# One fewer block-product pair in the first half-FFN, modulation weights loaded once for two conditions, and HGRN's states placed later, in a two-layer backbone on one core

## The chip, the cores and the metric

The kernel runs on one core of one Trainium2 chip, as one program. The metric is device time in microseconds, from the start of the program to its end, all loads from HBM and the stores of the result included. Times are medians of several runs.

## The reference, cut to what matters

Two layers work on a latent stream of 512 tokens and a context stream of 256 tokens, 1024 features each. A layer is a half-step FFN, a token mixer (HGRN2 in layer 0, a gated chunk MLP in layer 1) and a second half-step FFN. Each sub-layer's input is modulated, and its output is normalised, by rows of a modulation matrix product: nine chunks of 1024 values a layer, for the condition `c` of the latents (called "x" in the kernel) and, where context is needed, for `c_ctx` of the context (called "c").

```python
def modulation(cond, w_mod, b_mod):
    m = jax.nn.silu(cond) @ w_mod + b_mod          # w_mod: 1024 x 9*1024
    return m.reshape(m.shape[:-1] + (N_MOD, D_MODEL))
def modulate(x, m, k):
    return x * (1 + m[..., 3 * k + 1, :]) + m[..., 3 * k, :]
def post_norm_update(x, y, m, k, g, b):
    return layer_norm(DN_ALPHA * x + m[..., 3 * k + 2, :] * y, g, b)
def swiglu(h, w_in, w_out):                        # w_in: 1024 x 5632, w_out: 2816 x 1024
    gate, up = jnp.split(h @ w_in, 2, axis=-1)
    return (jax.nn.silu(gate) * up) @ w_out
...
        x = macaron_half_ffn(x, mx, 0, ...)        # chunks 0, 1, 2 for the latents
        ctx = macaron_half_ffn(ctx, mc, 0, ...)    # chunks 0, 1, 2 for the context
        hx = modulate(x, mx, 1)                    # chunks 3, 4
        yx, yc = hgrn2_mixer(hx, modulate(ctx, mc, 1), ...)
        x = post_norm_update(x, yx, mx, 1, ...)    # chunk 5
        x = macaron_half_ffn(x, mx, 2, ...)        # chunks 6, 7, 8
```

The mixer's scan has eight heads, two directions and 64-token chunks; each direction starts on the latents from the state that the context left.

## The kernel before

All products are float32, made from split operands: a value is a high part and a rest. `split` (L134 to L136) makes the high part on ACT (L135) and the rest on DVE (L136). `unit` (L139) loads one weight unit of 128x1024, 512 KB, into one of three `raw` buffers (L141) and splits it into one of six `w` buffers; the raw buffer is free when DVE's subtraction has read it. `mm3` (L146) issues three matmuls for each product of split operands (L148, L149, L150).

**The first half-FFN's input side** has 22 pairs of output blocks of 128 (gate and up). Three pairs run while the modulated input `xm` is still being made: the loop over the eight feature blocks k loads the modulation chunks 1 and 0 (`mw`, L1008) and one block of x (`xt`, three buffers, L1011), makes the dot products on DVE (L170), modulates on ACT (L1026), splits, copies the modulated block into spare `h` buffers for later use (L1039, two ACT copies of 128x256) and issues the matmuls. The other 19 pairs are made in `FeedSums.rest` (L766): first `plain` pairs, 48 matmuls of 512 columns each (`plain_pair`), then pairs by block products (`seven`, L673): seven products of 256 columns in place of eight, 84 matmuls of 256 columns, with four sums of weight halves on DVE and combinations of the results on DVE and ACT. During the plain pairs DVE and ACT also make the summed input blocks `f` that the block products need (`sum_steps`). Before, 9 pairs are plain and 10 are by blocks.

**The modulation rows** that are needed later are computed in the background. `mod_task` (L175) is a generator: each of its eight steps loads 512 KB of modulation weights (`mraw`, two buffers, L179) and makes a dot product on DVE for each condition it was given (L170, tile `junk`); after the last it finishes the chunk. Chunks 2, 5, 8 are gates: they go over a PE transpose (`pg`) and a store to HBM. `mod_step(n)` (L242) gives the queue of tasks n steps of credit, and is called after each pair or weight unit; `made(key)` (L255) runs as many steps as are missing. The loads go on SP's queue, which issues in order, as all loads and stores here do: a load that waits for its buffer holds all that is behind it.

**The stages, in order of time**: the start (`psf` matmuls while `xm` is made), the plain pairs, the block pairs, the output side of the first half-FFN for the latents (`OutPhase`, called x-out below), the input and output side of the same FFN for the context (ctx-in: 22 pairs of 48 matmuls of 256 columns; ctx-out: 22 units of 12 matmuls of 512 columns), HGRN's values, HGRN's heads, and what follows. The out phase of layer 0's second half-FFN (called (0,2) out phase below) calls `scraps` (L225) to queue modulation chunks (1,1) and (1,0) on other buffers (`rawu`).

**HGRN** runs eight heads in a loop (L1336 and on) that works on the projections of head h and on the scan of head h-1. `latent_states` (L1281) makes the three state products `pkl` of a direction; they need `kT`, a copy on ACT (L1235) of transposes that PE made just before. `gated` (L1324) transposes the normalised output `on` of a head (`pto`), which DVE makes at L1321.

The order of each engine's instructions comes from a scheduler that goes by the program's text; `tc.issue_after(i)` keeps an instruction behind i in that order.

Of the kernel before, what the change touches and what calls it, by code (L numbers as in the profile page):

```python
# [18 lines left out]
P = 128  # L19
D = 1024  # L20
KD = D // P
# [49 lines left out]
def backbone_kernel(  # L71
# [153 lines left out]
    def scraps(sp, l, chs, small=None):  # L225

        if small is None:
            s, small = (sp.tile([P, D], F32, tag="e", name="e", bufs=2) for _ in range(2))
        else:
            s, small = small[:, :D], small[:, D:]  # L230
        nc.sync.dma_start(s, cond[CI_OF["x"]].partition_broadcast(P))
        nc.scalar.activation(s, s, AF.Silu)
        small = Scraps(sp, small, "rawu")
        for ch in chs:
            queue_mod(small, {"x": s}, l, ch, ["x"])
# [751 lines left out]
    with sbuf(name="hp", bufs=1) as hp, sbuf(name="modp", bufs=1) as modp:  # L987
# [5 lines left out]
        with sbuf(name="first", bufs=1) as fp:  # L993
# [19 lines left out]

            staged, fed = 0, feed(0)
# [6 lines left out]
            for k in range(KD):  # L1021
# [15 lines left out]
                for p in range(2):  # L1037
                    b = f0.blocks[p, k // 2] if k % 2 else f0.block(p, k // 2)
                    nc.scalar.activation(b[:, k % 2, :], xf[:, p * 2 * P : (p + 1) * 2 * P], AF.Copy)  # L1039
# [4 lines left out]
                if k == 0:  # L1044
                    for _ in first:
                        pass
                elif k < 4:
                    f0.load((2, 2, 1)[k - 1])
            products(KD - 1, staged)
        nc.sync.dma_start(lnT, ln_T)  # L1050
        srow["c"] = silu_row(modp, "c")
        for ch, c in ((2, "x"), (1, "c"), (0, "c"), (4, "x"), (3, "x"), (2, "c"), (4, "c"), (3, "c")):
            queue_mod(modp, srow, 0, ch, [c])
        for l, ch in ((0, 5), (0, 7), (0, 6), (0, 8), (1, 2)):
            queue_mod(modp, srow, l, ch, ["x"])
        f0.enter()
        f0.sums()
        with sbuf(name="sp0", bufs=1) as sp:
            hget = f0.rest(hp, sp, 0.5, 9, 3.5)
        xcp = L0.enter_context(swap("xcp"))  # L1060
        xmc = new_xm(xcp, "xmc", TC)
        with bpools() as bp:
# [14 lines left out]
            ).run(bp, context_operand, 1.4)  # L1077
            hget = f1.rest(hp, 1.4)
# [8 lines left out]
            for l, ch in ((0, 8), (1, 2)):  # L1087
                made((l, ch, "x"))
# [3 lines left out]
    with sbuf(name="hgo", bufs=1) as hgo, ExitStack() as late:  # L1092
# [4 lines left out]
        with sbuf(name="hg", bufs=1) as hg:  # L1097
# [241 lines left out]
            for h in range(NH + 1):  # L1339
# [16 lines left out]
                if done:  # L1356
                    with tc.issue_after(last.ins):
                        gated(*done)
                if prev:
# [4 lines left out]
                    latent_states(h - 1, 1, r1, kT1)  # L1364
                if h < NH:
                    q, _ = proj_silu(h, 0, "q")
                    for r in (n0, n1):
                        queries(r, q)
                else:
                    op.lead(0, 2)  # L1370
                if prev:
# [22 lines left out]
    with sbuf(name="sp2", bufs=1) as sp, sbuf(name="hp2", bufs=1) as hp, bpools() as bp:  # L1394
# [11 lines left out]
        scraps(sp, 1, (1, 0))  # L1406
        op.run(bp, None, 1)
# [226 lines left out]
```

## Time and profile before

| | |
|---|---|
| median of 3 runs | 2460.67 us (2459.02 to 2461.65) |
| profiled execution | 2460.02 us, of which the trace's span is 2458.3 us |
| PE busy | 2413.8 us, 98% of the span |
| DVE, ACT busy | 2009.9 us (82%), 1190.7 us (48%) |
| DMA | 378.64 MB, mean 154 GB/s |
| start, plain pairs, block pairs | 54.2, 98.1, 102.2 us |
| x-out, ctx-in, ctx-out | 121.3, 141.7, 64.4 us |
| HGRN's heads 2 to 7 | 224.0 us |

Busy time of PE includes time in which matmuls overlap in the pipeline, so the share of 98% does not say that PE runs at its densest. The distance between the starts of two matmuls does: where nothing waits it is constant for a shape. A stage ends where the next one's first matmul starts.

### The profile page before, as it was taken

Reading aid. Unit: us, or ns where it says so; the run is one execution under the profiler, and the core shown is the slowest. Engines: PE = TensorE matmul, PEld = TensorE weight load, DVE = VectorE, ACT = ScalarE, POOL = GpSimd, SP = SyncE. Lnnn points to the kernel's source line nnn. Section 1 sums busy time; section 2 is a strip of 40 time slices with the busy share of each in tenths; the row PEclk is TensorE's granted clock in tenths of the full one; section 3 lists DMA queues with packets and bytes.
Section 4 is the critical chain, followed back from the end, with each engine's and each line's share of the span. In section 5 each row is a group of like instructions: output and inputs, shape, how many; then the busy total and the mean of one; then the engine's idle time right before and its main releaser. Section 6 shows DMA issues by size and latency. Waiting matters only on the chain.

```text
span 2458.3 us, 38793 instructions
## 1 busy us (share of the span) xinstructions
PE 2413.8 (98%) x15267; PEld 2198.5 (89%) x15267; DVE 2009.9 (82%) x3315; ACT 1190.7 (48%) x1878; POOL 35.0 (1%) x57
## 2 busy tenths in 40 slices
PE   7999999999999999999999999999999999999998
PEld 5889888988888888999988999988999988999987
DVE  7888889777388886988796988898899777998785
ACT  5335444444355542555643555534554443555641
POOL 0000000000000000000000000000000000000000
PEclk9999999999999999999999999999999999999999
DMA  8863866985211123433474333474422365333452
GB/s 316 276 206 120 284 213 219 314 301 178 86 61 61 47 66 116 138 119 106 130 239 139 112 114 108 147 253 139 133 89 87 114 222 173 135 121 104 138 160 80
DMA packets 110887, 378.64 MB, mean 154 GB/s; under 512 B 12856, under 2 KB 14192, under 8 KB 110704
## 3 DMA queue, kind: packets, MB, share of 16 engines
q1 hardware_dynamic: 110704, 376.17, 46.5%
q8 instruction: 119, 1.95, 0.3%
q14 instruction: 64, 0.52, 0.1%
HBM read 363.50 MB, written 12.61 MB: 153 GB/s over the span
## 4 chain that ended last, share of the span: by engine, by line
PE 72%; DVE 13%; DMA 7%; ACT 4%; issue 3%; POOL 1%; SPq 0%; DVEq 0%; POOLq 0%; ACTq 0%
PE y L150 7%; PE y L149 7%; PE y L148 7%; PE psc L148 6%; PE psc L150 6%; PE psc L149 6%; PE pse L150 3%; PE pse L148 3%; PE pse L149 3%; DVE w L136 3%; DMA mraw<-in_mod_w 3%; DMA raw<-in_ffn_w_out 2%; DVE junk L170 2%; ACT w L135 2%; DMA raw<-in_ffn_w_in 1%
## 5 line engine op out<-in xcount | busy, mean ns | idle before, releaser
L136 DVE TENSOR_TENSOR w<-raw,w 128x1024 fp32r<-128x1024 f32 (+3 forms) x447 | 495.2, 1113 | 142.8 <-ACT w L135 141.3
L135 ACT ACTIVATE w<-raw 128x1024 fp32r<-128x1024 f32 (+3 forms) x447 | 432.2, 970 | 370.5 <-DMA raw<-in_ffn_w_out 92.2
L150 PE MATMUL y<-w,hs 128*128 128x512 f32 x984 | 383.5, 390 | 2.4 <-DVE hs L136 2.3
L149 PE MATMUL y<-w,hs 128*128 128x512 f32 x984 | 382.9, 389 | 1.7 <-DVE w L136 1.7
L148 PE MATMUL y<-w,hs 128*128 128x512 f32 x984 | 383.7, 390 | 0.5 <-ACT w L135 0.5
L150 PEld LDWEIGHTS y<-w,hs 128*128 128x128 f32 x984 | 184.7, 188 | 44.1 <-DVE hs L136 5.6
L149 PEld LDWEIGHTS y<-w,hs 128*128 128x128 f32 x984 | 184.7, 188 | 40.4 <-DVE w L136 2.5
L148 PEld LDWEIGHTS y<-w,hs 128*128 128x128 f32 x984 | 184.8, 188 | 39.3 <-ACT w L135 0.7
L135 ACT ACTIVATE hs<-h 128x512 fp32r<-128x512 f32 (+1 forms) x220 | 123.8, 583 | 160.1 <-PE y L150 128.1
L148 PE MATMUL psc<-f,w 128*128 128x256 f32 x624 | 177.2, 284 | 1.6 <-ACT sc L734 1.5
L150 PE MATMUL pse<-f,w 128*128 128x256 f32 x624 | 176.9, 283 | 0.2 <-DVE w L136 0.2
L148 PE MATMUL pse<-f,w 128*128 128x256 f32 x624 | 176.7, 283 | 0.0
L150 PE MATMUL psc<-f,w 128*128 128x256 f32 x624 | 176.6, 283 | 0.0
L149 PE MATMUL pse<-f,w 128*128 128x256 f32 x624 | 176.6, 283 | 0.0
L149 PE MATMUL psc<-f,w 128*128 128x256 f32 x624 | 176.6, 283 | 0.0
L148 PE MATMUL psc<-xm,w 128*128 128x256 f32 x612 | 174.2, 285 | 0.9 <-ACT sc L734 0.9
L150 PE MATMUL psc<-xm,w 128*128 128x256 f32 x612 | 173.2, 283 | 0.0
L149 PE MATMUL psc<-xm,w 128*128 128x256 f32 x612 | 173.2, 283 | 0.0
L136 DVE TENSOR_TENSOR hs<-h,hs 128x512 fp32r<-128x512 f32 (+1 forms) x220 | 133.3, 632 | 42.3 <-ACT hs L135 41.9
L734 ACT ACTIVATE sc<-psc 128x256 f32<-128x256 f32 x218 | 83.5, 383 | 125.6 <-PE psc L150 119.6
L148 PE MATMUL psf<-xm,w 128*128 128x512 f32 (+1 forms) x384 | 127.4, 344 | 14.5 <-ACT xm L1032 11.1
L150 PE MATMUL psf<-xm,w 128*128 128x512 f32 (+1 forms) x384 | 130.4, 341 | 2.1 <-DVE w L136 2.1
(344 smaller groups left out, 6262.5 us busy)
## 6 DMA issues: line engine op xcount, KB each, us to landing
raw<-in_ffn_w_in SPq DMA_DIRECT2D x149, 512.0 KB, 4.7
raw<-in_ffn_w_out SPq DMA_DIRECT2D x110, 512.0 KB, 4.6
mraw<-in_mod_w SPq DMA_DIRECT2D x104, 512.0 KB, 5.0
rawu<-in_ffn_w_in SPq DMA_DIRECT2D x70, 512.0 KB, 3.7
rawu<-in_mod_w SPq DMA_DIRECT2D x64, 512.0 KB, 4.4
x<-x SPq DMA_DIRECT2D x36, 512.0 KB, 3.7
raw<-in_hg_wf SPq DMA_DIRECT2D x32, 512.0 KB, 3.6
raw<-in_cm_w_out SPq DMA_DIRECT2D x24, 512.0 KB, 4.5
```

Source lines behind the costliest of these rows:

```text
L135: latest_hi[0] = nc.scalar.activation(dst_hi, src, AF.Copy)
L136: latest[0] = nc.vector.tensor_tensor(dst_lo, src, dst_hi.bitcast(F32), ALU.subtract)
L148: nc.tensor.matmul(ps, ah, bh, start=start, stop=False, **kw)
L149: nc.tensor.matmul(ps, ah, bl, start=False, stop=False, **kw)
L150: return nc.tensor.matmul(ps, al, bh, start=False, stop=stop, **kw)
L170: nc.vector.scalar_tensor_tensor(junk, w[:, c], 1.0, s[:, c], ALU.mult, ALU.mult, dst[:, i : i + 1])
L734: nc.scalar.activation(sc[i], ps[:, :N2], AF.Copy, scale=scale)
```

## The change

- The first half-FFN takes 10 plain pairs and 9 by block products (before 9 and 10). The plain pairs give 2.7 steps of modulation each (before 3.5), the block pairs 0.4 (before 0.5).
- Chunks 2, 4 and 3 of layer 0 are queued once for both conditions ("xc"): one load of 512 KB serves two dot products. Before, each condition loaded them by itself. Chunk (0,8) is no longer in this queue; it is the first in the queue of the (0,2) out phase, whose rate goes from 1 to 1.25 steps a unit. The loads into `mraw` go from 104 to 72: 24 by sharing, 8 by the chunk that moves; those into `rawu` grow by these 8. The number of dot products is the same. The rates fall from 1.4 to 0.9 in x-out and from 1.4 to 0.5 in ctx-in; ctx-out keeps 0.5. At the end of ctx-in `made` runs the steps that chunks 5, 7 and 6 still lack. The loads of `mraw` that stand among ctx-out's weight loads go from 11 to 13, and nine of them stand among the first ten weight loads.
- At the start the copies into `h` (now `keep`) are made one k later, after the next block's high part.
- In HGRN, `latent_states` of the second direction is placed behind the first half of the next projection (`proj_silu`, tile `psq`); in the last turn of the loop, `gated` of head 6 is placed behind `op.lead(0, 2)`.

```diff
-    def scraps(sp, l, chs, small=None):
+    def scraps(sp, l, chs, small=None, first=None):
...
-        for ch in chs:
-            queue_mod(small, {"x": s}, l, ch, ["x"])
+        for key in ([first] if first else []) + [(l, ch) for ch in chs]:
+            queue_mod(small, {"x": s}, *key, ["x"])
...
+            def keep(k, x):
+                for p in range(2):
+                    b = f0.blocks[p, k // 2] if k % 2 else f0.block(p, k // 2)
+                    nc.scalar.activation(b[:, k % 2, :], x[:, p * 2 * P : (p + 1) * 2 * P], AF.Copy)
...
-                for p in range(2):
-                    b = f0.blocks[p, k // 2] if k % 2 else f0.block(p, k // 2)
-                    nc.scalar.activation(b[:, k % 2, :], xf[:, p * 2 * P : (p + 1) * 2 * P], AF.Copy)
+                if k:
+                    with tc.issue_after(latest_hi[0].ins):
+                        keep(k - 1, kept)
+                kept = xf
...
-        for ch, c in ((2, "x"), (1, "c"), (0, "c"), (4, "x"), (3, "x"), (2, "c"), (4, "c"), (3, "c")):
-            queue_mod(modp, srow, 0, ch, [c])
-        for l, ch in ((0, 5), (0, 7), (0, 6), (0, 8), (1, 2)):
+        for ch, conds in ((2, "xc"), (1, "c"), (0, "c"), (4, "xc"), (3, "xc")):
+            queue_mod(modp, srow, 0, ch, conds)
+        for l, ch in ((0, 5), (0, 7), (0, 6), (1, 2)):
             queue_mod(modp, srow, l, ch, ["x"])
...
-            hget = f0.rest(hp, sp, 0.5, 9, 3.5)
+            hget = f0.rest(hp, sp, 0.4, 10, 2.7)
...
-            ).run(bp, context_operand, 1.4)
-            hget = f1.rest(hp, 1.4)
+            ).run(bp, context_operand, 0.9)
+            hget = f1.rest(hp, 0.5)
...
-            for l, ch in ((0, 8), (1, 2)):
-                made((l, ch, "x"))
+            made((1, 2, "x"))
...
-                if done:
+                if done and h < NH:
                     with tc.issue_after(last.ins):
                         gated(*done)
...
-                    latent_states(h - 1, 1, r1, kT1)
                 if h < NH:
-                    q, _ = proj_silu(h, 0, "q")
+                    q, last = proj_silu(h, 0, "q")
+                    if prev:
+
+                        with tc.issue_after(last.ins):
+                            latent_states(h - 1, 1, r1, kT1)
                     for r in (n0, n1):
                         queries(r, q)
                 else:
+                    latent_states(h - 1, 1, r1, kT1)
                     op.lead(0, 2)
+                    gated(*done)
...
-        scraps(sp, 1, (1, 0))
-        op.run(bp, None, 1)
+        scraps(sp, 1, (1, 0), first=(0, 8))
+        op.run(bp, None, 1.25)
```

**On ACT, at the start**, from the first weight unit's first 128 columns on. Before:

```order
L135 ACTIVATE w<-raw 128x128
L1032 ACTIVATE xm<-xt,cols 128x512
L1039 ACTIVATE h<-xf 128x256 x2
L135 ACTIVATE w<-raw 128x896
L135 ACTIVATE w<-raw 128x1024
L1026 ACTIVATE xt<-xt,cols 128x512
```

Now:

```order
L135 ACTIVATE w<-raw 128x128
L1037 ACTIVATE xm<-xt,cols 128x512
L135 ACTIVATE w<-raw 128x896
L135 ACTIVATE w<-raw 128x1024
L1031 ACTIVATE xt<-xt,cols 128x512
L135 ACTIVATE w<-raw 128x1024
L135 ACTIVATE xm<-xt 128x512
L1017 ACTIVATE h<-xf 128x256 x2
```

The two copies into `h` of the first block moved from ahead of the first unit's other 896 columns to behind the second block's high part.

**On SP, in the middle of ctx-in**, among the weight loads of the context's input side. Before (buffer numbers are shown):

```order
L141 DMA raw_4389<-in_ffn_w_in 128x1024
L141 DMA raw_4419<-in_ffn_w_in 128x1024
L179 DMA mraw_4453<-in_mod_w 128x1024
L141 DMA raw_4457<-in_ffn_w_in 128x1024
L141 DMA raw_4487<-in_ffn_w_in 128x1024
L179 DMA mraw_4521<-in_mod_w 128x1024
L141 DMA raw_4525<-in_ffn_w_in 128x1024
L141 DMA raw_4555<-in_ffn_w_in 128x1024
L179 DMA mraw_4589<-in_mod_w 128x1024
L179 DMA mraw_4596<-in_mod_w 128x1024
```

Now:

```order
L141 DMA raw_4416<-in_ffn_w_in 128x1024
L179 DMA mraw_4544<-in_mod_w 128x1024
L141 DMA raw_4446<-in_ffn_w_in 128x1024
L141 DMA raw_4480<-in_ffn_w_in 128x1024
L179 DMA mraw_4676<-in_mod_w 128x1024
L141 DMA raw_4510<-in_ffn_w_in 128x1024
L141 DMA raw_4548<-in_ffn_w_in 128x1024
L141 DMA raw_4578<-in_ffn_w_in 128x1024
L416 DMA x_5046<-in_ctx_tok 128x1024
L141 DMA raw_4612<-in_ffn_w_in 128x1024
```

Four modulation loads to six weight loads became two to six, and the context's residual (`in_ctx_tok`) stands among them; before, both its loads stood at the end of the stage.

**On PE, in one HGRN head**, from the second direction's transposes (`ptk`) on; `pkl` are state products, `pssc` scores, `psq` the next head's projection. Before:

```order
L1233 MATMUL ptk<-ident,X 128x128 x3
L1287 MATMUL pkl<-v_5993,kT 128x128
L1287 MATMUL pkl<-v_5994,kT 128x128
L1287 MATMUL pkl<-v_5995,kT 128x128
L1256 MATMUL pssc<-B,X 128x128 x4
L1287 MATMUL pkl<-v_5996,kT 128x128
L1287 MATMUL pkl<-v_5995,kT 128x128
L1287 MATMUL pkl<-v_5994,kT 128x128
L148 MATMUL psq<-xm,w 128x512
```

Now (of the 24 matmuls of `psq` only the first and the last stand here):

```order
L1239 MATMUL ptk<-ident,X 128x128 x3
L1293 MATMUL pkl<-v_5847,kT 128x128
L1293 MATMUL pkl<-v_5848,kT 128x128
L1293 MATMUL pkl<-v_5849,kT 128x128
L1262 MATMUL pssc<-B,X 128x128 x4
L148 MATMUL psq<-xm,w 128x512
...
L150 MATMUL psq<-xm,w 128x512
L1293 MATMUL pkl<-v_5850,kT 128x128
L1293 MATMUL pkl<-v_5849,kT 128x128
L1293 MATMUL pkl<-v_5848,kT 128x128
```

The second group of `pkl` moved behind 24 matmuls of `psq`; the other 24 follow it.

## Rows read from the trace of the kernel before

**Rows 1.** The page: busy time of the engines as a share of the span, and the chain that ended last, by engine.

```profile
PE 2413.8 (98%) x15267; PEld 2198.5 (89%) x15267; DVE 2009.9 (82%) x3315; ACT 1190.7 (48%) x1878; POOL 35.0 (1%) x57
...
PE 72%; DVE 13%; DMA 7%; ACT 4%; issue 3%; POOL 1%; SPq 0%; DVEq 0%; POOLq 0%; ACTq 0%
```

**Rows 2.** Windows by stage: start and end in us, length, then busy us (and instructions) of PE, PEld, DVE, ACT and POOL, granted clock of PE, busy share of the DMA engines, GB/s. In order: plain pairs, block pairs, x-out, ctx-in, ctx-out, HGRN's heads 2 to 7.

```profile
54.20:152.30 98.10, 98.10 (x434) 81.04 (x434) 79.48 (x118) 30.57 (x39) 0.00 (x0) 1.00 0.79 259
152.30:254.50 102.20, 101.34 (x842) 100.91 (x841) 88.68 (x131) 59.65 (x103) 0.00 (x0) 1.00 0.44 144
254.50:375.80 121.30, 120.69 (x532) 98.85 (x531) 103.29 (x168) 50.64 (x73) 0.55 (x1) 1.00 0.76 253
375.80:517.50 141.70, 134.43 (x1090) 132.09 (x1088) 114.51 (x176) 58.15 (x82) 2.88 (x3) 0.99 0.81 275
517.50:581.90 64.40, 61.83 (x265) 49.05 (x266) 58.01 (x94) 38.20 (x65) 0.00 (x0) 1.00 0.86 289
...
722.70:946.70 224.00, 220.69 (x1359) 196.98 (x1358) 188.13 (x440) 110.99 (x173) 6.05 (x6) 1.00 0.19 57
```

**Rows 3.** Timeline of PE: start in us, us, engine, line, operation. Two starts of 512-column matmuls in the plain pairs, with four left out between them, and two of 256-column matmuls in the block pairs, with five left out.

```profile
99.97 0.39 PE L148 MATMUL psf<-xm,w 128*128 128x512 f32 x1
...
101.10 0.39 PE L150 MATMUL psf<-xm,w 128*128 128x512 f32 x1
...
199.76 0.28 PE L148 MATMUL psc<-f,w 128*128 128x256 f32 x1
...
200.48 0.28 PE L148 MATMUL psc<-f,w 128*128 128x256 f32 x1
```

**Rows 4.** PE's waits: what it waited for, us in total, times, longest. First ctx-in, then ctx-out.

```profile
PE psf L150 <- DVE w L136: 3.8, 6, 1.3
PE psf L148 <- ACT w L135: 2.8, 3, 1.6
...
PE y L150 <- DVE hs L136: 1.7, 3, 0.7
```

**Rows 5.** Windows, columns as in rows 2, of the change from x-out to ctx-in and of a stretch in ctx-out.

```profile
376.00:390.00 14.00, 14.00 (x122) 14.00 (x121) 13.28 (x26) 8.47 (x14) 2.88 (x3) 1.00 0.39 118
390.00:400.00 10.00, 9.52 (x81) 9.31 (x79) 9.92 (x19) 5.79 (x13) 0.00 (x0) 1.00 0.31 75
400.00:410.00 10.00, 7.89 (x53) 7.48 (x52) 9.52 (x14) 2.81 (x4) 0.00 (x0) 0.83 0.96 317
...
420.00:430.00 10.00, 8.53 (x69) 8.12 (x68) 9.43 (x16) 2.89 (x4) 0.00 (x0) 1.00 0.97 341
...
550.00:560.00 10.00, 8.88 (x38) 6.70 (x37) 10.00 (x19) 5.39 (x11) 0.00 (x0) 1.00 0.74 239
```

**Rows 6.** Waits of SP's queue in ctx-in: weight loads (L141) and modulation loads (L179), us in total, times, longest.

```profile
SPq L141 <- DVE w L136: 36.8, 21, 7.3
SPq L179 <- DVE junk L170: 27.7, 11, 7.4
```

**Rows 7.** DMA issues: count, KB each, median us from issue to landing. The first two in ctx-in, the third of the whole run (HGRN's weights, loaded where no modulation loads stand).

```profile
raw<-in_ffn_w_in SPq DMA_DIRECT2D x37, 512.0 KB, 5.5
mraw<-in_mod_w SPq DMA_DIRECT2D x27, 512.0 KB, 5.6
...
raw<-in_hg_wf SPq DMA_DIRECT2D x32, 512.0 KB, 3.6
```

**Rows 8.** DVE's instructions by line and form in ctx-in and ctx-out: count, busy us, mean ns, idle before.

```profile
L136 DVE TENSOR_TENSOR w<-raw,w 128x1024 fp32r<-128x1024 f32 x64 | 77.7, 1221 | 22.6 <-ACT w L135 22.0
L170 DVE SCALAR_TENSOR_TENSOR junk<-mraw,srow_x 128x1024 bf16<-128x1024 f32 x38 | 46.3, 1219 | 3.4 <-DMA mraw<-in_mod_w 3.1
L136 DVE TENSOR_TENSOR hs<-h,hs 128x256 fp32r<-128x256 f32 x44 | 17.2, 416 | 1.4 <-ACT hs L135 1.4
```

**Rows 9.** Timeline of PE in an HGRN head, and near the loop's end; in brackets the idle time before, and what ended it.

```profile
804.39 0.83 PE L1287 MATMUL pkl<-v,kT 128*128 128x128 f32 x6
805.06 1.06 PE L1256 MATMUL pssc<-B,X 128*128 128x128 f32 x8
806.49 0.94 PE L1287 MATMUL pkl<-v,kT 128*128 128x128 f32 x6 [0.38 <-ACT kT L1235]
...
942.05 0.63 PE L1327 MATMUL pto<-ident,on 128*128 128x128 f32 x4 [1.03 <-DVE on L1321]
```

**Rows 10.** PE's waits in HGRN's heads 2 to 7, columns as in rows 4.

```profile
PE pkl L1287 <- ACT kT L1235: 2.3, 6, 0.4
```

**Rows 11.** The start: timeline of ACT, DVE and SP, then PE's wait for the rest parts and SP's wait for an `xt` buffer.

```profile
10.91 0.71 ACT L1039 ACTIVATE h<-xf 128x256 f32<-128x256 f32 x2
12.49 1.09 DVE L136 TENSOR_TENSOR w<-raw,w 128x896 fp32r<-128x896 f32 x1 [0.76 <-ACT w L135]
...
41.17 0.63 ACT L135 ACTIVATE xm<-xt 128x512 fp32r<-128x512 f32 x1
44.89 0.63 ACT L135 ACTIVATE xm<-xt 128x512 fp32r<-128x512 f32 x1
46.23 1.06 ACT L161 ACTIVATE srow_c<-srow_c 128x1024 f32<-128x1024 f32 x1
...
SPq L1011 <- DVE xm L136: 12.1, 3, 4.4
```

**Rows 12.** Windows, columns as in rows 2, of a stretch in the (0,2) out phase.

```profile
1240.00:1280.00 40.00, 40.00 (x178) 33.14 (x177) 38.83 (x60) 16.58 (x23) 0.00 (x0) 1.00 0.83 270
```

More of the change, by code (lines that the diff above doesn't have):

```diff
@@ L1048, in backbone_kernel @@
                     f0.load((2, 2, 1)[k - 1])
+            keep(KD - 1, kept)
             products(KD - 1, staged)
```

## The prediction, made before the changed kernel was timed

> **What bounds the kernel now.** The page comes first: PE is busy for 98% of the span, and the chain that ended last is PE's for 72%, with 13% of DVE and 7% of DMA in it [rows 1]. So PE sets the time nearly everywhere. Next comes the pace of PE where nothing waits: five matmuls of 512 columns in 101.10 - 99.97 = 1.13 us, 0.226 us each, and six of 256 columns in 0.72 us, 0.120 us each [rows 3]. With these the windows by stage [rows 2] show where PE falls behind. The 432 matmuls of the plain pairs, 98.10/432 = 0.227 each, leave nothing to win. The block pairs need 840 x 0.120 = 100.8 of 102.20 us. Ctx-in needs 1090 x 0.120 = 130.8 of 141.70: 10.9 us are lost. Ctx-out needs 265 x 0.227 = 60.2 of 64.40: 4.2 are lost. These two are the worst stages that the change touches. HGRN's heads idle for 224.00 - 220.69 = 3.3 us. What ends PE's idle time in ctx-in is the weight split, on ACT and DVE [rows 4]; what stands behind that is a late load: the DMA engines are busy for 0.81 of the stage and 0.96 to 0.97 in parts of it [rows 2, 5], a weight load lands after 5.5 us where it took 3.6 without modulation loads around [rows 7], and SP holds weight loads for up to 7.3 us and modulation loads, with all that is behind them, for as long [rows 6].
>
> **The change part by part.** The sum is made against the profiled execution, 2460.02 us; the median of the three runs lies 0.65 above it, and that is added at the end.
>
> *One plain pair for a block pair.* PE gains 48 matmuls of 0.227 and loses 84 of 0.120: 10.9 - 10.1 = +0.8 us. By stages, 98.10/9 - 102.20/10 gives +0.7. DVE and ACT get lighter here, but PE does not wait for them in this stage, so that is worth nothing. I take +0.8. The Trainium skill ("TensorE: Matmul & The Clock Gate", section "Wait — 56ns, not 53.3ns?") gives 215.7 ns for a warm matmul of 512 columns, and by its formula one of 256 takes 109.2; an estimate from this page for the exchange is 10.35 - 9.17 = +1.2 us. The row's paces are both some 0.01 us longer than the page's, and the row decides.
>
> *Dots and loads around the plain and block pairs.* DVE is busy for 79.48 of 98.10 us with 3.5 dots a pair; by my count the 27 steps on 10 pairs now carry about 38 dots, 3.8 a pair. At 1.22 us a dot [rows 8] that is 0.4 us more in 10.9, from 0.81 to 0.84 busy. In the block pairs it goes from 0.5 dots to 0.8 a pair, from 0.87 to 0.90. PE's lead covers both: 0. If it does not, DVE's growth in the block pairs, 9 x 0.3 x 1.22 = 3.3 us, bounds the loss.
>
> *X-out.* In its first half a unit of 5.4 us now carries 1.8 dots (0.9 steps for two conditions) for 1.4: +0.49 us of DVE, which stands at 103.29 of 121.30, so 0.85 becomes 0.94 there. The nearest row of a DVE as full is ctx-out: 0.90 busy and 4.2 us lost, though part of that is the loads'. I take +0.5, from 0 to +3. The DMA share falls, from 0.76.
>
> *Ctx-in and ctx-out.* Ctx-in issues 27 modulation loads beside 37 weight loads [rows 7]; now some ten. A weight buffer goes round in landing + high part + rest, 5.5 + 1.0 + 1.2 = 7.7 us, three buffers give a unit every 2.6 us, and PE eats one in 24 x 0.120 = 2.88. That leaves 0.3 us a unit, which one hold of 7.3 us on SP uses up for 24 units. At the landing time of 3.6 a unit comes every 1.9 us, and PE can be led by all six `w` buffers. So I expect ctx-in's loss to go nearly whole. At its beginning, between 376 and 410, DVE is 95 to 99% busy and DMA at 0.31 to 0.39 up to 400: there it is DVE, with norms, operands and dots, that holds SP [rows 5]. By the order of SP's loads some seven modulation loads fewer stand around it now, 7 x 1.22 = 8.5 us of DVE; I leave 2 of the 10.9 us. In ctx-out the loads are not fewer (13 for 11), and nine fall on the first ten units, where DVE then needs 1.22 + 2 x 0.42 + 1.22 = 3.3 us for PE's 2.7. That deficit, 9 x 0.6 = 5 us, is met by the lead brought from ctx-in, up to five units or 13 us of PE. The loss at the start of the stage goes, that around the evacuation (DVE 10.00 of 10.00 at 550, rows 5) stays: 2.2 of the 4.2. Together -8.9 - 2.0 = -10.9 us. Bounds: -6 if the beginning's 4.3 us (2.6 idle and 1.7 of granted clock, 0.83 for ten us at 400) and all of ctx-out's stay; -14 if nearly nothing does.
>
> *HGRN.* The second `pkl` group follows 1.43 us after the start of eight matmuls (`pssc`) that at the pace of the group before (six in 0.67) take 0.89 [rows 9]: 0.54 lost, in six heads [rows 10], 3.2 us. Behind half of `psq`, 5.4 us later, `kT` has long been copied, and `pkl`'s results are needed only in the next head. The `pto` of the last turn waited 1.03 for `on` and now has `op.lead` ahead of it: 1.1. Together -4.3; bounds -5 and 0, see the rivals.
>
> *The start.* Taking the two copies out of ACT's way brings the first unit's rest part forward by up to 0.7 us: DVE waited 0.76 for it [rows 11]. Against that, an `xt` buffer now is read last by a copy that stands behind the next block's high part, 44.89 - 41.17 = 3.7 us later, so the next-but-two x load is issued later, and SP's queue behind it too; SP waits for such a buffer already, 4.4 us at the longest. The scheduler has put a modulation load more ahead of one of these x loads, which lessens it. The last `xm` high part now also stands behind the Silu of `srow_c`, whose load comes late on SP. I take +0.5, from -0.6 to +3 (one such step shown on PE, less the gain).
>
> *Chunk (0,8) in the (0,2) out phase.* DVE is at 38.83 of 40 there already [rows 12], PE without a gap. A quarter step a unit adds about 0.3 us of DVE to 5.4, 2.4 us over the window, of which 1.2 is free. I take +0.5, from 0 to +2.5.
>
> Sum: 0.8 + 0 + 0.5 - 10.9 - 4.3 + 0.5 + 0.5 = -12.9, so 2447.1 for a run like the profiled one, and **2447.8 us** against the median.
>
> **The rivals.** (a) *Loads were not the cause in ctx-in.* If PE waits there because DVE and ACT work through a backlog left by x-out, and not for DMA, the loss stays: the sum without -10.9 is -2.0, 2458.7 us. For it: DVE is nearly full between 376 and 430 [rows 5]. Against it: over all of ctx-in DVE is at 114.51 of 141.70 and ACT at 58.15 [rows 2], so a backlog should be worked off early, and fewer dots shorten it too. The Trainium skill speaks for it ("DMA: Bandwidth & Descriptors", section "Specifications": 435 GB/s as the fabric's ceiling): at that rate 512 KB take 1.2 us, and an estimate from this page for 1.7 loads a unit is 2.05 us of PE's 2.88, no limit. The rows show 317 to 341 GB/s at shares of 0.96 to 0.97 [rows 5], 1.54 us a load and 2.6 a unit, so the trace stands closer to the limit than the page. Chance 0.09.
>
> (b) *HGRN's gap only moves.* DVE meets the state steps of the second direction where they now stand, waits there for `pkl`, and the splits and scores queued behind come late, so that PE loses in another place what it won at `kT`. For it: DVE is 188.13 of 224.00 busy in the heads. Then the sum is -8.6, 2452.1 us. Chance 0.13.
>
> (c) *Slower: the shared loads hold SP.* Each of the 24 shared loads keeps its `mraw` buffer for a second dot, 24 x 1.22 = 29.3 us in all. With two buffers, SP's next modulation load waits that long, and weight loads stand behind it; plain pairs and x-out, both dense or nearly so now, would show it as PE waiting for `w`. All of it on PE makes -12.9 + 29.3 = +16.4, 2477 us; it ends above the time before by 0.2% (4.9 us) from 17.8 of the 29.3 us on. Against it: PE's lead of up to six units absorbs holds of a few us. The same page (section "Anatomy of one DMA — SWDGE (gpsimd) path") says that a semaphore wait takes place on the issuing sequencer before dispatch, which is the holding that rows 6 show. Chance 0.04.
>
> (d) *The start loses more than it wins*, 3 us, by the late x loads: 2450.3 us, within the likeliest case's sign. Chance 0.10.
>
> **How the numbers follow.** My forecast has 0.64. All terms at their better ends give -0.6 + 0.7 - 14 - 5 = -19, 2442; with single terms at their worse ends and (b) or (d) it comes to 2455. The range is 2440 to 2455; it leaves out (a), (c) and some of the tails. A measurement of this kernel can tell about 0.2%, 4.9 us, from no change: faster means below 2455.7. (b), (d) and the forecast with nearly all its tails lie below: 0.86. (a) lies within: with the tails 0.10. Slower 0.04, rival (c).
>
> **What would show it.** Ctx-in's window near 133 us for its matmuls, with the granted clock at 1.00 at 400, a landing time of weight loads near 4 us, and SP's waits for `junk` mostly gone; ctx-out near 62. In the heads, no idle PE ahead of `pkl`, and the six heads at 220 to 221 us. The plain pairs at 10.9 each, with no wait for `w`. Wrong would be: PE still waiting for `w` in ctx-in with DMA idle (rival a); new waits of `psq` or `po` in the heads (b); waits for `w` in the plain pairs or x-out (c); a start over 56 us (d); waits for `hs` in the first half of ctx-out or in the (0,2) out phase, where DVE is asked for more than it has.

## The result, and the profile after

The changed kernel took 2445.28 us (median of 4 runs, 2443.93 to 2448.79) where the kernel before took 2460.56: a ratio of 0.9941, with an interval of 0.9923 to 0.9958. In five further runs it took 2447.06 against 2459.39, 0.9950 (0.9937 to 0.9962). Forecast were 2447.8 us and a gain of 12.9; measured are 15.3 and 12.3. The first profiled execution was the slowest of its four, 2448.79 us with a span of 2447.1: against the trace of before it shows 11.2 us of gain. Its mean granted clock of TensorE was 0.997, that of the other three 0.999; where the clock was lost in the profiled run is seen below.

The windows by stage of the changed kernel, columns as in [rows 2]: plain pairs, block pairs, x-out, ctx-in, ctx-out, and the stretch of HGRN that answers to the row 722.70:946.70 of before (from the same distance behind the same matmuls; the four `pto` matmuls of the last turn, some 0.5 us, now stand behind its end).

```profile
54.32:163.37 109.05, 109.05 (x483) 90.18 (x482) 94.42 (x143) 33.82 (x42) 0.00 (x0) 1.00 0.75 246
163.37:254.08 90.71, 90.71 (x757) 90.70 (x756) 76.31 (x112) 53.17 (x91) 0.00 (x0) 1.00 0.38 117
254.08:373.79 119.71, 119.71 (x530) 99.11 (x529) 102.73 (x170) 51.19 (x73) 0.55 (x1) 1.00 0.66 212
373.79:506.26 132.47, 131.12 (x1090) 130.46 (x1089) 102.58 (x149) 61.27 (x86) 2.87 (x3) 1.00 0.78 251
506.26:575.03 68.77, 64.58 (x267) 50.97 (x266) 55.40 (x94) 35.09 (x61) 0.00 (x0) 0.95 0.71 234
715.03:934.66 219.63, 219.24 (x1355) 196.12 (x1354) 187.71 (x440) 110.44 (x172) 6.05 (x6) 1.00 0.19 58
```

Put beside [rows 2], the first three stages are now at the pace of their matmuls without a gap, ctx-in is 9.2 us shorter, HGRN's stretch 4.4, and **ctx-out is 4.4 us longer**, with a granted clock of 0.95 and 4.2 us of idle PE. What PE waits for is in its waits, first ctx-in, then ctx-out, to be read beside [rows 4] (`y` are the sums of the out phase, `hs` the split hidden blocks that they are made from):

```profile
PE psf L150 <- DVE w L136: 1.3, 3, 0.8
...
PE y L150 <- DVE hs L136: 4.2, 3, 2.3
```

The wait for `hs` stands at two places; the timelines of PE and of DVE there show what DVE did instead:

```profile
514.83 0.50 PE L150 MATMUL y<-w,hs 128*128 128x512 f32 x1 [2.30 <-DVE hs L136]
...
517.29 0.79 PE L150 MATMUL y<-w,hs 128*128 128x512 f32 x1 [1.50 <-DVE hs L136]
...
518.31 0.63 PE L149 MATMUL y<-w,hs 128*128 128x512 f32 x1
518.74 0.63 PE L150 MATMUL y<-w,hs 128*128 128x512 f32 x1
...
511.80 0.16 DVE L198 SCALAR_TENSOR_TENSOR mc_x<-acc_x,mbT 128x8 f32<-128x8 f32 x1
511.99 0.17 DVE L272 TENSOR_TENSOR opc<-opc,mc_x 128x8 f32<-128x8 f32 x1
512.08 1.22 DVE L136 TENSOR_TENSOR w<-raw,w 128x1024 fp32r<-128x1024 f32 x1
513.22 1.22 DVE L170 SCALAR_TENSOR_TENSOR junk<-mraw,srow_x 128x1024 bf16<-128x1024 f32 x1
514.36 0.08 DVE L170 DVE_READ_ACCUMULATOR junk<-mraw,srow_x 128x1 f32 x1
514.36 0.42 DVE L136 TENSOR_TENSOR hs<-h,hs 128x256 fp32r<-128x256 f32 x1
515.67 1.23 DVE L170 SCALAR_TENSOR_TENSOR junk<-mraw,srow_x 128x1024 bf16<-128x1024 f32 x1 [0.89 <-DMA mraw<-in_mod_w]
516.82 0.08 DVE L170 DVE_READ_ACCUMULATOR junk<-mraw,srow_x 128x1 f32 x1
516.82 0.42 DVE L136 TENSOR_TENSOR hs<-h,hs 128x256 fp32r<-128x256 f32 x1
```

The last of the steps that `made` forces (L198 finishes a chunk at 511.80) and the first of ctx-out's stand ahead of `hs` on DVE, and DVE even waits 0.89 us for the load of such a step while PE waits for the 0.42 us behind it. After it the clock falls, and two matmuls of 512 columns start 0.43 us apart (518.31 and 518.74) where 0.227 is the pace; windows of 5 us:

```profile
511.00:516.00 5.00, 2.50 (x9) 1.18 (x8) 4.07 (x9) 1.06 (x3) 0.00 (x0) 1.00 0.94 300
516.00:521.00 5.00, 3.71 (x9) 2.93 (x10) 4.31 (x8) 3.29 (x6) 0.00 (x0) 0.54 0.94 329
521.00:526.00 5.00, 5.00 (x19) 4.04 (x18) 2.20 (x5) 1.19 (x3) 0.00 (x0) 0.78 0.83 278
```

PE was idle for 2.5 of five us, and then ran nearly all of the next five at 1.2 in place of 2.4 GHz (0.54). Over the time that PE was busy the clock took 3.71 x 0.46 + 5 x 0.22 = 2.8 us on top of the idle time; the wait and its clock, 4.2 + 2.8 us, cost more than the stage's old stalls, 4.2.

In an HGRN head the wait for `kT` of [rows 9, 10] is gone: the scores are followed by `psq` at once, and the second `pkl` group costs its six matmuls.

```profile
722.72 1.06 PE L1262 MATMUL pssc<-B,X 128*128 128x128 f32 x8
723.54 0.47 PE L148 MATMUL psq<-xm,w 128*128 128x512 f32 x1
...
729.11 0.83 PE L1293 MATMUL pkl<-v,kT 128*128 128x128 f32 x6
729.69 0.48 PE L148 MATMUL psq<-xm,w 128*128 128x512 f32 x1
```

### The profile page after: what moved, and what is told of

It reads as the page before. It is cut to its first block, busy times and chain, and to the rows that moved or that the text cites. A ratio compares the mean times of both kernels' runs of the same rounds, so it can differ in the third digit from the quotient of the medians.

```text
span 2447.1 us, 38641 instructions
## 1 busy us (share of the span) xinstructions
PE 2411.1 (99%) x15231; PEld 2196.9 (90%) x15231; DVE 2003.1 (82%) x3306; ACT 1188.5 (49%) x1871; POOL 34.1 (1%) x57
## 4 chain that ended last, share of the span: by engine, by line
PE 82%; DVE 8%; DMA 5%; ACT 2%; issue 2%; POOL 1%; SPq 0%; DVEq 0%; POOLq 0%; ACTq 0%
PE y L150 8%; PE y L149 8%; PE y L148 8%; PE psc L148 6%; PE psc L150 6%; PE psc L149 6%; PE pse L150 3%; PE pse L148 3%; PE pse L149 3%; DMA raw<-in_ffn_w_in 2%; PE psf L149 2%; PE psf L150 2%; PE psf L148 2%; DVE w L136 2%; PE psa L150 1%
## 5 line engine op out<-in xcount | busy, mean ns | idle before, releaser
L148 PE MATMUL psc<-f,w 128*128 128x256 f32 x616 | 174.8, 284 | 0.9 <-ACT sc L734 0.9
L150 PE MATMUL pse<-f,w 128*128 128x256 f32 x616 | 174.6, 283 | 0.2 <-DVE w L136 0.2
L148 PE MATMUL pse<-f,w 128*128 128x256 f32 x616 | 174.3, 283 | 0.0
L150 PE MATMUL psc<-f,w 128*128 128x256 f32 x616 | 174.3, 283 | 0.0
L149 PE MATMUL psc<-f,w 128*128 128x256 f32 x616 | 174.3, 283 | 0.0
L149 PE MATMUL pse<-f,w 128*128 128x256 f32 x616 | 174.3, 283 | 0.0
L148 PE MATMUL psc<-xm,w 128*128 128x256 f32 x604 | 171.9, 285 | 0.6 <-ACT sc L734 0.6
L149 PE MATMUL psc<-xm,w 128*128 128x256 f32 x604 | 170.9, 283 | 0.0
L150 PE MATMUL psc<-xm,w 128*128 128x256 f32 x604 | 170.9, 283 | 0.0
L148 PE MATMUL psf<-xm,w 128*128 128x512 f32 (+1 forms) x400 | 134.7, 345 | 14.5 <-ACT xm L1037 11.1
L150 PE MATMUL psf<-xm,w 128*128 128x512 f32 (+1 forms) x400 | 136.4, 342 | 2.1 <-DVE w L136 2.1
```

The lines of the kernel that those rows point to most:

```text
L148: nc.tensor.matmul(ps, ah, bh, start=start, stop=False, **kw)
L149: nc.tensor.matmul(ps, ah, bl, start=False, stop=False, **kw)
L150: return nc.tensor.matmul(ps, al, bh, start=False, stop=stop, **kw)
```

## The experiments

Times are medians; ratios are to the kernel before, run beside it on the same chip. That kernel's median there was 2460.10 us for experiments 1, 2 and the first kernel of 4, 2459.39 for the repeated kernel, the first kernels of 5 and 6 and experiment 7, and 2458.74 for 3 and the second kernels of 5 and 6; between these groups the ratios are to be compared, not the times. "Ctx-in" and "ctx-out" are the distances between the same first matmuls in each profile, as in the windows above.

**1. HGRN's placement alone**, put into the kernel before (`latent_states` behind `proj_silu` and `gated` behind `op.lead(0, 2)`, as in the diff of the change).

> The kernel before with the placement of HGRN's states and of head 6's gated output alone. Theory (the second pkl group waited for its kT copy, and behind half of psq the copy is done; pto waited for on): the six heads 2 to 7 go from 224.0 to some 220.3 us, no wait of pkl for kT is left, and the time falls by 4 to 5 us to about 2456. Rival (the gap only moves, the saving in the changed kernel came from elsewhere): the time stays within 1.5 us of 2460.6.

2456.46 us, ratio 0.9986 (0.9977 to 0.9995): 3.6 us less than the 2460.1 of before. From the second to the eighth head's first score matmul it took 221.1 us before, and now, by the window of this run,

```profile
715.94:933.50 217.56, 217.56 (x1334) 194.48 (x1333) 186.45 (x430) 112.21 (x176) 6.07 (x6) 1.00 0.19 59
```

217.56: PE without a gap. The theory holds, with 3.6 us in the heads and in the time, a little under its 4 to 5. The gap did not move. From the eighth head's score matmul to the next FFN's first matmul this run took 56.5 us, the kernel before 56.8, the changed kernel 57.1: the wait of `pto` for `on` is gone, but its 1.0 us does not come out of the whole stretch.

**2. Two more loads in each of ctx-in's steps** of the changed kernel, and **two more dots**:

```diff
 def mod_task(...):
     ...
+            for _ in range(extra[0]):          # 2 during ctx-in's pairs, else 0
+                more = modp.tile([P, D], F32, tag="mraw", name="mraw", bufs=2)
+                nc.sync.dma_start(more, mod_w[l, ch, f])
```

```diff
+            for _ in range(extra[0]):
+                spare = modp.tile([P, 1], F32, tag="spare", name="spare", bufs=1)
+                mod_dot(modp, spare, raw, srow["x"])
```

> The changed kernel with two more loads of 512 KB, which nothing reads, in each of ctx-in's modulation steps: some 27 to 30 modulation loads beside the weight loads as before the change, with the few dot products of after. It does work that the result does not need. Theory (late loads were what PE waited for in ctx-in): ctx-in goes from 132.5 back to 139 to 142 us, and the time to 2451 to 2455. Rival (DVE's and ACT's backlog was): ctx-in stays below 135 us and the time below 2448.

> The changed kernel with two more dot products, whose sums nothing uses, in each of ctx-in's modulation steps, on the weights that are loaded anyway: DVE's dots of before the change with the few loads of after. It does work that the result does not need. Theory (loads): ctx-in stays below 135 us and the time below 2448. Rival (DVE's backlog): ctx-in goes back to 139 to 142 us, the time to 2451 to 2455.

With the loads 2460.61 us, ratio 1.0003 (0.9994 to 1.0011): all of the gain is lost, and ctx-in takes 148.2 us, more than before. With the dots 2451.81, ratio 0.9965 (0.9951 to 0.9979): 6.5 us more than the changed kernel's first median, ctx-in 137.4. Ctx-in, first with the loads, then with the dots:

```profile
374.33:522.51 148.18, 133.97 (x1091) 133.13 (x1089) 101.06 (x149) 58.44 (x82) 2.87 (x3) 0.95 0.80 278
373.96:511.38 137.42, 133.65 (x1090) 133.09 (x1089) 122.99 (x188) 61.16 (x84) 2.87 (x3) 0.98 0.73 238
```

Neither theory stands as it was written: loads cost most, but dots are not free. The place is telling too. With the loads, the input pairs lost some 5 us until the lead was used up, and then PE waited once, for the first unit of ctx-out:

```profile
512.29 0.28 PE L150 MATMUL psf<-xmc,w 128*128 128x256 f32 x1
522.51 1.22 PE L148 MATMUL y<-w,hs 128*128 128x512 f32 x2 [9.93 <-ACT w L135]
```

Three loads in a row are not the old spacing, and there are 33 modulation loads in this ctx-in where the kernel before has 27. With two `mraw` buffers modulation loads now also wait for each other: from 480 to 523 us SP waited 10.3 + 5.2 us for earlier ones to land. So this run shows what loads can cost when they hold the queue, not what the old ones did cost, and the same question was put to the kernel before, by taking away.

**3. The kernel before without ctx-in's dots, and without its loads.**

```diff
-                mod_dot(modp, accs[c][:, f, :], raw, srow[c])
+                n = 8 if less[0] else D               # less[0] during ctx-in's pairs
+                mod_dot(modp, accs[c][:, f, :], raw[:, :n], srow[c][:, :n], n)
```

```diff
-            raw = modp.tile([P, D], F32, tag="mraw", name="mraw", bufs=2)
-            nc.sync.dma_start(raw, mod_w[l, ch, f])
+            if less[0]:
+                raw = held[0]
+            else:
+                raw = held[0] = modp.tile([P, D], F32, tag="mraw", name="mraw", bufs=2)
+                nc.sync.dma_start(raw, mod_w[l, ch, f])
```

> The kernel before, with ctx-in's modulation dots made over 8 of 1024 columns: all loads stay where they were, DVE's dots there all but go. The sums of these chunks leave out the other columns. Theory (after the last runs: late loads and DVE's dots both make PE wait in ctx-in, the loads more): ctx-in falls from 141.7 (138.3 in another run of the same stage) to 135 to 138 us. Loads alone: no change, 138 to 142. DVE alone: 131 to 133.

> The kernel before, with ctx-in's modulation loads left out: the dots stay where they were and read the weights loaded last, so that their sums are those of other rows. Theory (both, the loads more): ctx-in falls to 132 to 134 us. Loads alone: 131 to 133. DVE alone: no change, 138 to 142.

Without the dots 2454.0 us, ratio 0.9983 (0.9972 to 0.9995), 4.7 us less; without the loads 2447.91, ratio 0.9959 (0.9946 to 0.9973), 10.8 less, of 2458.74. Ctx-in and ctx-out, first without dots, then without loads:

```profile
377.15:513.06 135.91, 131.81 (x1090) 130.57 (x1089) 86.51 (x177) 58.52 (x83) 2.87 (x3) 1.00 0.82 290
513.06:575.69 62.63, 61.32 (x267) 49.26 (x266) 57.55 (x94) 37.73 (x63) 0.00 (x0) 1.00 0.86 289
...
377.43:510.81 133.38, 131.04 (x1091) 130.41 (x1090) 120.32 (x183) 62.40 (x86) 2.88 (x3) 1.00 0.68 214
510.81:571.01 60.20, 60.20 (x268) 49.50 (x266) 52.76 (x88) 35.88 (x60) 0.00 (x0) 1.00 0.78 248
```

Without the loads PE idles 2.3 us in ctx-in and not at all in ctx-out, though DVE is busy for 120.32 of 133.38. Without the dots the DMA engines stay at 0.82 and 0.86, and 4.1 us of idle PE remain in ctx-in. So both together, by the medians the loads more than twice as much. The two do not come apart wholly: without the dots a modulation buffer comes free earlier, and SP's waits for `junk` fall from 27.7 us [rows 6] to 14.6, so that some of the dots' share is again loads that are held. Ctx-out, where nothing was taken away, is freed by the lead that ctx-in builds up: eight of its weight loads stand in ctx-in without the modulation loads, three before.

**4. Ctx-in's rate**: 0.8 steps a pair, so that `made` forces nothing; and the changed kernel itself once more, to see whether its wait is an accident.

```diff
-            hget = f1.rest(hp, 0.5)
+            hget = f1.rest(hp, 0.8)
```

> The changed kernel with 0.8 steps of modulation a pair in ctx-in in place of 0.5, so that no step is left for the forced run at its end. Theory (the new idle time at the start of ctx-out comes from the forced steps' dot products, which stand on DVE ahead of the hidden blocks' splits hs): ctx-out's wait of y for hs, 4.2 us in the changed kernel, falls below 1.5, its window goes from 68.7 to some 62 to 63 us with a granted clock of 1.00, ctx-in stays within 1.5 us of 132.5, and the time is 2441 to 2444 us. Rival (ctx-out is short of loads and DVE time anyway, wherever the five steps stand): ctx-out stays above 66 us or ctx-in loses what ctx-out wins, and the time stays at 2445 to 2446.

> The changed kernel itself, once more. In its first profile the granted clock was 0.82 and 0.84 in the first 24 us of ctx-out, and that execution was 3.5 us slower than the median of its runs. Theory (PE's wait for hs of some 4 us stands in every run, the clock's fall behind it only in some): median 2444 to 2447 us; the profile shows y waiting for hs again, 3 to 5 us, whether or not the clock falls. Rival (the first profile's wait is an accident too): no wait for hs over 1 us.

With 0.8: 2444.22 us (five runs, 2443.29 to 2445.86), ratio 0.9936 (0.9924 to 0.9949). Ctx-out falls to 61.7 us at a clock of 1.00, with 0.6 us of wait for `hs`; ctx-in takes 134.4, more than the theory allowed:

```profile
374.31:508.68 134.37, 131.06 (x1090) 130.41 (x1089) 105.80 (x158) 60.82 (x85) 2.88 (x3) 1.00 0.78 266
508.68:570.36 61.68, 61.05 (x267) 49.27 (x266) 51.21 (x84) 37.05 (x63) 0.00 (x0) 1.00 0.69 218
```

In the profiles the two stages together go from 201.2 (again: 199.0) to 196.1, but the median is only 1 to 3 us lower, and the intervals of the ratios meet: in the time of the whole kernel the gain is not shown. The repeated kernel waits again, 3.4 us for `hs` at 514 to 517, and its clock falls to 0.66 in the next five us:

```profile
516.00:521.00 5.00, 4.45 (x13) 3.57 (x14) 4.30 (x8) 3.40 (x6) 0.00 (x0) 0.66 0.93 321
```

No accident, then, though its size varies.

**5. Steps elsewhere.** In x-out (1.1 a unit, 0.55 in ctx-in), or late in ctx-in:

```diff
-            ).run(bp, context_operand, 0.9)
-            hget = f1.rest(hp, 0.5)
+            ).run(bp, context_operand, 1.1)
+            hget = f1.rest(hp, 0.55)
```

```diff
-            hget = f1.rest(hp, 0.5)
+            hget = f1.rest(hp, 0.4, 8, 1.1)       # 0.4 for eight pairs, then 1.1
```

> The changed kernel with 1.1 steps a unit in x-out for 0.9 and 0.55 in ctx-in for 0.5, so that no step is left for the forced run. Theory (x-out runs at the pace of its matmuls with room left on DVE, and ctx-in has fewer loads at its beginning than with 0.8): x-out stays at 119.7 to 120.5 us, ctx-in comes to 132 to 133.5, ctx-out to 62, and the time to 2442 to 2444 us. Rival (two dots a step fill DVE in the first half of x-out: 1.22 + 1.37 + 2.2 x 1.22 = 5.3 of 5.44 us): x-out takes 121.5 to 124 us, and the time is 2445 or more.

> The changed kernel with ctx-in's steps given late: 0.4 a pair for eight pairs, then 1.1, so that none is left for the forced run. Theory (the idle PE at 395 to 421 us of the kernel with 0.8 throughout, 3.8 us, comes from steps that fall into the change from x-out to ctx-in, where DVE and SP are behind): ctx-in 131.5 to 132.5 us, ctx-out 61.5 to 62.5, time 2441 to 2443, below all kernels so far. Rival (late steps meet ctx-out's loads instead): ctx-out 64 or more, time 2444 or more.

More in x-out: 2443.71 us, ratio 0.9934 (0.9920 to 0.9947). Its rival was right on the stage, 122.95 us in x-out: PE waits once, 2.7 us for `hs` at 320, at the turn of the halves, where DVE works off a backlog, the evacuation and the context's operand together (5.00 of 5.00 us busy from 320 on):

```profile
320.00:325.00 5.00, 2.28 (x10) 1.46 (x9) 5.00 (x10) 2.40 (x4) 0.00 (x0) 1.00 0.37 138
325.00:330.00 5.00, 5.00 (x24) 4.10 (x23) 5.00 (x9) 1.27 (x2) 0.00 (x0) 1.00 0.50 129
```

The first half, where the rival had placed the loss, kept its 59.9 us. After this wait the clock did not fall. Ctx-in at 131.7 and ctx-out at 61.9 pay for the stage, and the time stays below the rival's 2445. Late in ctx-in: **2440.53 us** (six runs, 2437.63 to 2441.59), ratio 0.9930 (0.9914 to 0.9946). All its runs lie below every run of the changed kernel, but on a chip where the kernel before is faster too; by the ratio it is 0.1 to 0.2% ahead, and the intervals meet. Its two stages take 192.25 us, with 18 modulation loads in ctx-in where the changed kernel has 14:

```profile
374.73:505.63 130.90, 130.53 (x1091) 130.31 (x1089) 108.62 (x160) 62.45 (x86) 2.87 (x3) 1.00 0.80 278
505.63:566.98 61.35, 60.56 (x267) 49.42 (x266) 49.43 (x83) 35.65 (x60) 0.00 (x0) 1.00 0.65 210
```

More loads than in the changed kernel's ctx-in, and 7 to 9 us less than in its two profiles: where the steps stand decides, once there are few enough. A step's load and its dot move together here, so this run does not say which of the two the place matters for.

**6. Nine plain and ten block pairs** on the kernel with 0.8, first with rates that give the same steps, then with the change's own.

```diff
-            hget = f0.rest(hp, sp, 0.4, 10, 2.7)
+            hget = f0.rest(hp, sp, 0.36, 9, 3.0)      # then: 0.4, 9, 2.7, with 0.9 in ctx-in
```

> The kernel with 0.8 steps a pair in ctx-in, with 9 plain and 10 block pairs as before the change and rates that give the same steps (3.0 and 0.36). Theory (both kinds are dense, so the exchange costs what its matmuls take): plain and block pairs together take 0.8 us less than with 10 and 9 (198.95 against 199.76), and the time is 0.5 to 1 us below that kernel's 2444.2, near 2443.4. Rival (the tenth block pair costs DVE time or a gap at the change from plain to block pairs, 1.4 us of which stood in the kernel before): no gain, 2444 to 2445.5.

> Nine plain and ten block pairs with the change's rates of 2.7 and 0.4 (the run with 3.0 lost 6.3 us where PE's transposes of the gate chunk waited for DVE), and 0.9 in ctx-in. Theory (the rate sets DVE's backlog in the plain pairs, two dots a step): no wait of pg, plain 98.1 us and block pairs 100.8, time 0.5 to 1 us below the 2444.2 of ten and nine pairs with 0.8 in ctx-in. Rival (with nine plain pairs the sums of the inputs and the ten pairs' weight sums crowd DVE whatever the rate): pg waits 2 us or more again, plain over 100 us, time 2445 or more.

With 3.0: 2447.76 us, 3.5 more than with ten and nine (3.6 more than experiment 7's kernel, run beside it), against the theory. The plain pairs took 105.1 us, 7 above their matmuls. PE's timeline has one gap, and the window about it shows DVE full and the clock down:

```profile
87.42 0.39 PE L150 MATMUL psf<-xm,w 128*128 128x512 f32 x1
92.70 0.27 PE L191 MATMUL pg<-ident,acc_x 128*8 128x128 f32 x1 [4.89 <-DVE acc_x L189]
...
88.00:99.00 11.00, 5.98 (x21) 4.71 (x22) 11.00 (x21) 2.12 (x2) 0.00 (x0) 0.84 0.77 261
```

The transpose of gate chunk 2, shared now, stands in PE's queue ahead of the pairs' matmuls, and waits for DVE, which is still at the chunk's double dots. In the changed kernel the same transposes come at 97.8 us without a wait. With 2.7 the wait is gone, and plain and block pairs take 98.2 + 100.9 = 199.0 us against 199.8 with ten and nine: the exchange itself costs 0.7 us, as the matmuls say. The whole, 2447.01 us, is not faster: x-out takes 120.6 us, and ctx-out 67.0, with a wait at its start again. This time no step is forced there (chunk 6 is finished at 498.9, ctx-out begins at 506.6). ACT waits for a weight load that lands late, and the high part of `hs` stands behind that weight in its order:

```profile
PE y L148 <- ACT hs L135: 3.0, 1, 3.0
...
512.42 1.06 ACT L135 ACTIVATE w<-raw 128x1024 fp32r<-128x1024 f32 x1 [3.13 <-DMA raw<-in_ffn_w_out]
```

Its rates differ from those of the runs beside it, so only the stages are compared.

**7. The copies `keep` back at their old place**, on the kernel with 0.8:

```diff
-                if k:
-                    with tc.issue_after(latest_hi[0].ins):
-                        keep(k - 1, kept)
-                kept = xf
+                keep(k, xf)
```

> The kernel with 0.8 steps a pair in ctx-in, with the copies into h back at their old place at the start. Theory (the move neither wins nor costs more than half a microsecond: the start took 54.3 us before and after): start 54.0 to 54.8 us, time within 1 us of 2444.2. Rival (the move hides a gain of 0.7 that a late x load takes away again): PE's waits at the start differ in place, the first unit's rest part coming 0.6 us later, and the x loads earlier, with the sum the same or 1 us shorter.

2444.12 us against 2444.22, start 54.2 us. The time of the whole kernel is the same within what it can tell. The start tells more, over all profiles: with the copies late it took 54.3 to 55.6 us in nine of them, 54.9 on average; with the copies early 54.1 to 54.4 in five, 54.3 on average, and on each chip every early one is below every late one. So the move seems to cost some 0.6 us; four of the five early ones are kernels that differ in other ways too.

## Why the prediction was right, and where its terms were not

The time came out 2.5 us below the forecast in the first set of runs and 0.7 in the second, within the range. By its steps, with the sizes from the profiles. For stages that an experiment left as they were before there is more than one profile of the old code (experiments 1 and 3):

- **Plain for block pair**, +0.8: right for the matmuls. Dense, 199.8 us against 198.9 before the change (98.08 + 100.79 in experiment 1's run), and 0.7 between experiments. But three of four profiles of the old code held 0.9 to 1.4 us of gaps in the block pairs (the waits are shown under x-out), and with the change they are gone; the profiled kernel's trace even shows a gain of 0.5. "PE does not wait for them in this stage" was wrong by that much: [rows 2] showed 102.20 us for 100.8. The rows' 0.227 and 0.120 held. The estimate of +1.2 from the paces in the Trainium skill ("TensorE: Matmul & The Clock Gate", section "Wait — 56ns, not 53.3ns?") did not: no run here shows 215.7 ns for 512 columns.
- **Dots around the plain pairs**, 0: right at the change's rate, and for a thin reason. DVE is full there (11.00 of 11.00 us in the windows from 55 to 88 of the changed kernel). At 3.0 on nine pairs, experiment 6, it cost 7 us with the clock: rival (c)'s shared loads, by another door than the one described. Not a weight load behind a held buffer made PE wait, but a transpose in PE's own queue, behind DVE.
- **X-out**, forecast +0.5, measured -1.6 (the old code took 121.3 to 123.3 us in four profiles): wrong in sign. I had counted the first half, where the dots become denser, and it held (119.71 us in all seven profiles with ten plain pairs and this rate). The second half, where 1.4 single dots became 0.9 and where the kernel before had its waits, I left out. Before, PE's waits from the plain pairs to the end of x-out were, in the block pairs and in x-out:

```profile
PE psc L148 <- ACT sc L734: 0.9, 2, 0.6
PE y L150 <- DVE hs L136: 0.6, 1, 0.6
```

- **Ctx-in**, -8.9: measured -9.2, between the two first profiles. The old code took 138.3 us in experiment 1's profile and the repeated kernel 132.2, so the gain is 5.9 to 9.5 us, and that it met the forecast so closely is chance. The cause was the loads, with the dots behind them (experiments 2 and 3), so rival (a) is out as a whole, though the dots had up to 5 us in it. Two steps of the argument failed. SP's waits for `junk` did not mostly go, there are 14 modulation loads in the window, not some ten, and one wait is as long as before:

```profile
SPq L179 <- DVE junk L170: 16.1, 10, 7.4
```

  And landing did not go to 4 us. Weight loads still land after 5.3 us (5.5 before), and the DMA engines are at 0.78 (0.81), since the weights now run ahead, six of ctx-out's among them (three before). Without modulation loads it was 4.5. So the loads that stood in the queue ahead of the weights starved PE, and not the landing time of each weight; how much of that was their number and how much their place was not taken apart.
- **Ctx-out**, -2.0: the wrong step of the sum, +4.4 in the first profile and +2.4 in the second (+0.6 if that is put beside experiment 1's 66.2 of the old code). The two stages together gave 3.2 to 7.2 us of the forecast 10.9. "That deficit is met by the lead brought from ctx-in" is what failed: the lead was in weights, but `hs` cannot be made before the hidden blocks, and on DVE it stands behind the forced dots. I named the waits for `hs` as what would show me wrong, and gave the range no room for them nor for the clock behind them. Experiment 4 shows the cause: without the forced steps the stage takes 61.7 us. It is not the only one. Of the six kernels without forced steps five took 60.2 to 62.3 us, but the last of experiment 6 took 67.0, for a late weight load.
- **HGRN**, -4.3: the heads 3.6 (forecast 3.2), the last `pto` not to be seen in the whole: its wait of 1.0 us did not come out of the time, and no run shows where it went. Rival (b) is out.
- **The start**, +0.5, and **chunk (0,8)**, +0.5: +0.1 and +0.1 between the first profiles. Over all profiles the start cost some 0.6 (experiment 7), as forecast, and rival (d)'s 3 us is out. In the (0,2) out phase DVE was at 38.29 of 40 us in the same stretch, not above it.

That the sum came out near is partly luck: x-out's two us and the block pairs' gaps on one side and ctx-out's four to six on the other stand against each other. What stays open: why the median of the first four runs lies 3.5 us below their profiled one. The mean clock, 0.997 against 0.999 of 2447 us, is some 5 us by these rounded figures, and the fall behind the wait is 2.8 of them; but the other three runs left no rows, so where they kept their clock is not shown. Whether the sharing by itself, at the old rates, would have given ctx-in's gain was not tried.

## What to carry to other kernels

Loads that nobody is waiting for still cost when they share an in-order queue with loads that somebody will wait for: share or drop them first, then look at where they stand; in the profiles, four more steps in a better place beat four fewer (experiment 5). A background task whose remains are forced at a deadline put them here at a place where PE had no slack; give it a rate that leaves none, and let it rise once the next stage has its lead. In a stage without a gap, look for the engine that is full though nothing waits yet: there a rate changed by a tenth cost more than the matmuls that were at stake (experiment 6). And profile a stage twice before taking a gain of a few us in it for the change's: the same ctx-in differed by 3.4 us from one profile to the other.

## What was not expected of the hardware

The granted clock fell to 0.54 of a 5 us window after PE had been idle for 2.5 us of the five before (0.66 in the repeated run), and a stall of 10 us brought 0.95 as the mean of a whole stage of 65 us. So a short wait in a dense stage can cost half its length or more again in clock (2.8 us behind 4.2 in the first profile). It need not: after a single wait of 2.7 us in x-out (experiment 5) the clock stayed at 1.00, and no run here shows what decides it. And a load of 512 KB landed hardly sooner with a seventh fewer bytes moved in the stage (33.23 MB after 38.93), after 5.3 us instead of 5.5.
